# Loading x and the first weights on one queue, and adding and scaling several tiles at once at the end, in a two-layer recurrent decoder on one core

## The chip, the cores and the metric

The kernel runs on one core of a Trainium2 chip. The core has five engines that run side by side: PE (TensorE, matmuls, with weight loads shown as PEld), DVE (VectorE), ACT (ScalarE), POOL (GpSimd) and SP (SyncE, which here only issues transfers). The metric is the device time of one execution in microseconds (us), as a median over runs. TensorE's granted clock is 0.998 over the profiled execution.

## The reference, cut to what matters

The input x is 256 positions of 2048 features, float32. Two layers follow each other, each with a gated convolutional FFN behind it, and a last norm:

```python
for layer in range(DEPTH):                       # DEPTH = 2
    if layer % 2 == 0:
        x = rglru_rwkv7_layer(x, even_norm[e], even_w_in[e], ...)
    else:
        x = mlstm_layer(x, odd_norm[o], odd_w_in[o], ...)
    x = conv_ffn(x, ffn_norm[layer], ffn_w_gate[layer], ffn_w_up[layer], ...)
return rms_norm(x, final_norm)

def rms_norm(x, g):
    y = x32 * lax.rsqrt(jnp.mean(x32 * x32, axis=-1, keepdims=True) + EPS)
    return (y * g).astype(x.dtype)

def conv_ffn(x, norm, w_gate, w_up, conv_w, conv_b, w_down):
    h = rms_norm(x, norm)
    u = jax.nn.silu(causal_dwconv(h @ w_gate, conv_w, conv_b)) * (h @ w_up)
    return x + u @ w_down
```

The even layer normalizes x and multiplies it by `even_w_in`; its last 288 output columns are the low-rank inputs of the RWKV-7 half (decay, in-context rate and gate), and the kernel computes these first. All else of the layers is untouched by the change.

## The kernel before, in words

**Layout.** Features lie on the 128 partitions and the 256 positions along the free axis, so x is 16 tiles of 128 x 256, called the residual: one buffer `res_sb` of 128 x 16 x 256, whose tiles are `res[k]`.

**Precision.** Every float32 operand is split in two: a rounded part made by ACT (a copy or a scaled copy) and the remainder made by DVE (a subtraction). A product takes the rounded weights with both parts of x, and the weights' remainder with the rounded part of x. Lines 254 and 255 split weights (`wh`, `wl` from `raw`), lines 378 and 379 make the operands `x` of the residual and multiply the norm's gain in. The factor 1/rms comes only behind the matmuls: it is one value for each position, the square sums are gathered in `ssq` (ACT squares at L392, DVE adds at L394), two small matmuls (L405) add them over the partitions, POOL raises to the power -1/2 (L416), two more matmuls (L432) spread the result over all partitions, and ACT copies it to `rstd` (L434, shown as `bc`).

**Weights** come from memory in chunks of up to 1 MB into the tile `raw`, which has two buffers, all issued by SP. A chunk can be issued only when its buffer has been read out by the split.

**The start.** The constructor loads the constants `con` (identity and ones) on POOL's queue. `load_x` (L148) loads the gain vector and then x on ACT's queue, in pieces of 1, 1, 2, 4, 4 and 4 tiles (L160, L163), and beside it the low-rank weights `elow` on SP's queue: group 0 in three pieces (L161), groups 1, 2 and 3 whole (through `raw_load`, L235). A group holds the weights of four k-tiles, 4 x 288 columns. Behind group 1 SP loads the vectors (`vec`, L192). `warm(7)` runs seven matmuls on zeros, two instructions each (L146), and then come 16 k-tiles of three products of three matmuls each (L270 to L272, outputs `pc`, `pc`, `pw`). Behind that the program loads `con_even` (L512, recorded at L204) on SP and begins the wide projection of the even layer (weights `ein`, output `mm`, the same lines). For each of the eight head groups j it loads `lora` (L542: on SP for j = 0, else POOL), `a_w` (L544, POOL) and, inside the head group's own sequence, `gate` (L753, POOL). The work of `gate` for j = 0 begins with an ACT cast at L805, that of `lora` at L610.

**Order.** The program text gives the order only as a preference. A scheduler walks through it, and an engine (or a queue) takes the first instruction in the text that can go; one that must wait for a buffer is passed by later ones. The order on each engine that comes out is fixed and cannot change at run time.

**The FFN** (L472) has an up-projection (`flat_pairs` over `fgu`, L346 and L348) and a down-projection (`fd`, same lines), which yields one pair of output tiles after another: a PSUM tile of 128 x 2 x 2 x 256, the first 2 for the two output tiles, the second 2 for the two parts that are to be added. For each tile `add_residual` (L465) adds both parts to the residual on DVE (L467), makes the next layer's operand (not in the last FFN) and the square; in the last FFN ACT then scales the tile by the final gain (L372).

**The end.** Behind the last pair come the square sum, the power and the spread, and then a loop over the 16 tiles (L1171): two of three tiles are multiplied by `rstd` on DVE and the third on POOL, and each time three tiles are done SP stores them (L1174), the last tile alone.

Of the kernel before, what the change touches and what calls it, by code (L numbers as in the profile page):

```python
# [17 lines left out]
F32 = mybir.dt.float32  # L18
F32R = mybir.dt.float32r
AF = mybir.ActivationFunctionType  # L20
ALU = mybir.AluOpType
# [3 lines left out]
P = 128  # L25
T = 256
D = 2048
KD = D // P
# [87 lines left out]
class Builder:  # L116
    def __init__(self, tc, io, ctx):
        self.tc, self.nc, self.io = tc, tc.nc, io
        self.tile_pool = lambda **k: tc.tile_pool(reuse_waits="tile", **k)
        nc = self.nc  # L120
        self.n = 0
        pool = lambda name, bufs, **k: ctx.enter_context(self.tile_pool(name=name, bufs=bufs, **k))
        self.const = pool("const", 1)
        self.raw = pool("raw", 2)
        self.parts = pool("parts", 2)

        self.short = pool("short", 1)
        self.act = pool("act", 1)
        self.mm_ps = pool("mm_ps", 3, space=PSUM)
        self.vec_sb = self.const.tile([P, NV], F32, name="vec_sb")  # L130
        self.cons = {}
        self.load_con("con", self.const)
        self.x = [None] * KD
        self.sumsq = None
        self.rstd = None
        self.tasks = []
        self.norm_psum = lambda: self.psum_mm()[:, 0]

    def warm(self, n):

        nc = self.nc
        z = self.act.tile([P, 2 * T], F32, name="warm", tag="x15")
        nc.vector.memset(z, 0.0)
        ps = self.psum_mm()
        for i in range(n):
            nc.tensor.matmul(ps, z[:, 0:P], z, start=True, stop=True)  # L146

    def load_x(self, gain, low, outs):  # L148

        nc = self.nc  # L150
        res = self.act.tile([P, KD, T], F32, name="res")
        self.res_sb = res
        self.res = [res[:, k] for k in range(KD)]
        g = VOFF[gain]
        nc.scalar.dma_start(out=self.vec(gain, 0, KD), in_=self.io["vec"][:, g:g + KD])
        w = sum(n for _, n in outs)
        first = [0, 1, 2, 4]
        raw = self.raw_tile(4 * w)
        for a, b in zip(first, first[1:]):
            nc.scalar.dma_start(out=res[:, a:b], in_=self.io["xT"][:, a:b])  # L160
            nc.sync.dma_start(out=raw[:, a * w:b * w], in_=low[0][:, a * w:b * w])  # L161
        for i in range(1, 4):
            nc.scalar.dma_start(out=res[:, 4 * i:4 * i + 4], in_=self.io["xT"][:, 4 * i:4 * i + 4])  # L163
        self.warm(7)
        for i in range(4):
            raw = raw if i == 0 else self.raw_load(low[i], 4 * w)
            if i == 1:
                self.load_vec(gain)
            hi, lo, piece = self.parts_of(raw, 4)
            for k in range(4 * i, 4 * i + 4):  # L170
                self.operand(k, gain)
                piece(k % 4)
                c = k % 4 * w
                for ps, n in outs:
                    self.mm3(ps[0:n], (hi, lo), slice(c, c + n), self.x[k], k == 0, k == KD - 1)
                    c += n
        self.rstd = None
        self.start(self.squares())
# [188 lines left out]
    def norm_tile(self, k, gain):  # L367
        if gain is not None:
            self.operand(k, gain)
        self.square(k)  # L370
        if gain is None:
            self.nc.scalar.activation(self.res[k], self.res[k], AF.Copy, scale=self.vec("final_norm", k))  # L372

    def operand(self, k, gain):
        nc, a = self.nc, self.act
# [89 lines left out]
    def add_residual(self, m, ps, gain):  # L465
        for i in range(2):
            self.nc.vector.tensor_tensor(out=self.res[m], in0=ps[:, i], in1=self.res[m], op=ALU.add)  # L467
        if gain is not False:
            self.norm_tile(m, gain)


    def ffn(self, l, gain):  # L472
        nc, tc = self.nc, self.tc
        with ExitStack() as es:
# [15 lines left out]
                ux.append(big.tile([P, 2, T], F32R, name=self.name("ux"), tag=f"u{f}"))  # L490
                self.split(u, ux[f])
            for m, ps in enumerate(self.flat_pairs(self.io[f"fd{l}"], NF, KD // 2, ux, pps)):
                for i in range(2):
                    self.add_residual(2 * m + i, ps[:, i], gain)


    def even(self, gain):
        nc, tc = self.nc, self.tc
        with ExitStack() as es:
# [10 lines left out]
            low = [(self.pc(P, T), P), (self.pc(P, T), P), (self.pw(P, T), 32)]  # L510
            self.load_x("even_norm", self.io["elow"], low)
            self.load_con("con_even", E, nc.sync)  # L512
            ps = self.projections(ein, 40, EWIDE)
# [24 lines left out]
            ps = chain([ahead], ps)  # L538
            pairs, lru = [], []
            for j in range(8):  # L540
                lw = self.wt("lora", P, 2, P, bufs=1)
                (nc.gpsimd if j else nc.sync).dma_start(out=lw, in_=self.io["lora"][j, :, 0:2])  # L542
                lru_w = self.wt("lru_w", P, 2, P, bufs=1)
                nc.gpsimd.dma_start(out=lru_w, in_=self.io["a_w"][j])  # L544
                k, r, v = (self.shifted(self.W, next(ps), 3 + 3 * j + i, t)
                           for i, t in enumerate("krv"))
                if j == 0:
# [48 lines left out]
    def rwkv_pair(self, j, lw, low, r, k, v, out):  # L596

        nc = self.nc
# [34 lines left out]
        ps = self.pw(P, T)  # L633
# [116 lines left out]
            V.tensor_tensor(out=tt, in0=ps, in1=zt, op=ALU.add)  # L750
            yield from wait(WAITS[8])
        gw = once("gate", P, 2, P)
        nc.gpsimd.dma_start(out=gw, in_=self.io["lora"][j, :, 2:])  # L753

        ps = self.pw(P, NCK, 2, CHUNK)
        for c in range(NCK):
# [397 lines left out]
    def build(self):  # L1154
# [11 lines left out]
        self.norm_psum = lambda: self.psum_mm()[:, 0]  # L1166
        self.norm_end()
        self.finish(*self.tasks)
        for k in range(KD):
            e = nc.gpsimd if k % 3 == 2 else nc.vector  # L1170
            e.tensor_tensor(out=self.res[k], in0=self.res[k], in1=self.rstd, op=ALU.mult)  # L1171
            if k % 3 == 2 or k == KD - 1:
                o = k - k % 3
                nc.sync.dma_start(out=self.io["out"][:, o:k + 1], in_=self.res_sb[:, o:k + 1])  # L1174


@with_exitstack
# [108 lines left out]
```

## Time and profile before

| | us |
|---|---|
| median of three runs | 2606.73 |
| lowest and highest | 2604.91, 2606.99 |
| the profiled execution | 2604.45 |
| its span | 2602.6 |
| PE busy in it | 2567.6 |
| DVE, ACT, POOL busy | 1869.0, 1470.6, 142.5 |
| moved between memory and chip | 454.41 MB |

The profile is of one execution. A row of a group or of the timeline reads: start and busy time in us, engine, line of the kernel, operation, what it writes and reads by the program's names, shape, count, and in brackets the idle time of the engine just before and what ended it. PE's spans are modelled and overlap: what counts is the distance from one start to the next. SPq, ACTq and POOLq are the engines' instruction queues, where transfers are issued. A row of transfers gives the issuing queue, the count, the size of one and the median time from issue to landing. In the chain of waits a row is start, length and what ran; a row with DMA is a transfer from issue to landing. Only the ends of the span are looked at here: about the first 50 us, and the 17 us behind the last large matmul.

### The profile page before, as it was taken

The page shows a single profiled execution, that of the slowest core. Times are in us where ns is not written, and L with a number is a line of the kernel's source. Part 1 is how long each engine was busy: PE and PEld are TensorE (multiplying, and loading weights), DVE is VectorE, ACT ScalarE, POOL GpSimd, SP SyncE. Part 2 cuts the span into 40 slices and gives each one's busy share as a digit, 9 for nine tenths or more (in the row PEclk, how much of TensorE's full clock was granted, in tenths as well). Part 3 has the DMA queues.
Part 4 walks back from the last instruction along what each step waited for, and adds up shares of the span by engine and source line. Part 5 has one row for each costly group of instructions (what it writes and reads, how often), then busy time and mean ns, then how long its engine had stood idle before and what let it go on. Part 6 is the DMA issues. An engine that isn't in the chain of part 4 may idle for free.

```text
span 2602.6 us, 43142 instructions
## 1 busy us (share of the span) xinstructions
PE 2567.6 (99%) x16438; PEld 2264.4 (87%) x16438; DVE 1869.0 (72%) x4205; ACT 1470.6 (57%) x3071; POOL 142.5 (5%) x402
## 2 busy tenths in 40 slices
PE   9999999999999999999999999999999999999997
PEld 8888887888888888888888888888888888888886
DVE  7988888988777775555777788865677777775554
ACT  7766663655555554444666777644555555554443
POOL 1222121000000000000010000000000000000000
PEclk9999999999999999999999999999999999999999
DMA  6434334565555555555444344455555555555553
GB/s 210 158 109 139 122 105 148 181 221 207 190 187 191 193 194 194 195 179 197 162 147 146 130 146 164 144 197 192 185 189 193 194 194 194 187 188 192 191 197 130
DMA packets 67696, 454.41 MB, mean 175 GB/s; under 512 B 9328, under 2 KB 10352, under 8 KB 14240
## 3 DMA queue, kind: packets, MB, share of 16 engines
q1 hardware_dynamic: 62064, 441.69, 48.8%
q0 software_dynamic: 4416, 7.85, 1.1%
q8 instruction: 129, 2.11, 0.3%
q10 hardware_dynamic: 1008, 2.11, 0.2%
q14 instruction: 79, 0.65, 0.1%
HBM read 448.70 MB, written 2.10 MB: 173 GB/s over the span
## 4 chain that ended last, share of the span: by engine, by line
PE 79%; issue 11%; DVE 6%; ACT 2%; DMA 1%; POOL 1%; ACTq 0%; DVEq 0%; POOLq 0%
PE mp L346 30%; PE mm L333 20%; PE mp L348 15%; PE mm L270 2%; PE mm L271 1%; PE mm L272 1%; PE mm L268 1%; DVE wl L255 1%; PE mm L266 1%; PE sc L986 1%; PE pv L971 1%; PE pz L1126 1%; DMA blocks<-dc 1%; PE pr L980 0%; POOL rsq L416 0%
## 5 line engine op out<-in xcount | busy, mean ns | idle before, releaser
L255 DVE TENSOR_TENSOR wl<-raw,wh 128x512 fp32r<-128x512 f32 (+1 forms) x1680 | 1092.0, 684 | 521.3 <-ACT wh L254 517.9
L254 ACT CAST wh<-raw 128x512 fp32r<-128x512 f32 (+1 forms) x1680 | 955.5, 617 | 696.2 <-PE mp L346 530.2
L346 PE MATMUL mp<-x,wh 128*128 128x512 f32 x2816 | 874.1, 392 | 0.0
L348 PEld LDWEIGHTS mp<-x,wl 128*128 128x128 f32 x2816 | 528.8, 188 | 116.4
L348 PE MATMUL mp<-x,wl 128*128 128x256 f32 x2816 | 555.7, 279 | 0.0
L346 PE MATMUL mp<-ux,wh 128*128 128x512 f32 x1408 | 436.8, 392 | 0.0
L346 PEld LDWEIGHTS mp<-x,wh 128*128 128x128 f32 x2816 | 426.5, 188 | 0.1
L333 PE MATMUL mm<-x,wh 128*128 128x512 f32 x1024 | 333.8, 406 | 0.0
L348 PEld LDWEIGHTS mp<-ux,wl 128*128 128x128 f32 x1408 | 264.4, 188 | 58.1
L348 PE MATMUL mp<-ux,wl 128*128 128x256 f32 x1408 | 277.9, 279 | 0.0
L333 PEld LDWEIGHTS mm<-x,wl 128*128 128x128 f32 x1024 | 192.2, 188 | 42.8 <-issue 0.2
L346 PEld LDWEIGHTS mp<-ux,wh 128*128 128x128 f32 x1408 | 213.2, 188 | 0.0
L333 PE MATMUL mm<-x,wl 128*128 128x256 f32 x1024 | 205.8, 280 | 0.0
L270 PE MATMUL mm<-x,wh 128*128 128x256 f32 x640 | 188.8, 295 | 0.0
L272 PE MATMUL mm<-x,wl 128*128 128x256 f32 x640 | 179.2, 280 | 1.8 <-DVE wl L255 1.8
L271 PE MATMUL mm<-x,wh 128*128 128x256 f32 x640 | 179.5, 281 | 0.0
L333 PEld LDWEIGHTS mm<-x,wh 128*128 128x128 f32 x1024 | 158.9, 188 | 5.3 <-ACT z L459 2.7
L333 PE MATMUL mm<-yx,wh 128*128 128x512 f32 x512 | 160.4, 392 | 0.0
L270 PEld LDWEIGHTS mm<-x,wh 128*128 128x128 f32 x640 | 120.1, 188 | 6.5 <-issue 0.9
L272 PEld LDWEIGHTS mm<-x,wl 128*128 128x128 f32 x640 | 120.0, 187 | 2.4 <-DVE wl L255 2.2
L271 PEld LDWEIGHTS mm<-x,wh 128*128 128x128 f32 x640 | 120.3, 188 | 0.7
L333 PEld LDWEIGHTS mm<-yx,wl 128*128 128x128 f32 x512 | 96.2, 188 | 19.9
(362 smaller groups left out, 2752.3 us busy)
## 6 DMA issues: line engine op xcount, KB each, us to landing
raw<-fgu SPq DMA_DIRECT2D x176, 1024.0 KB, 4.8
raw<-fd SPq DMA_DIRECT2D x88, 1024.0 KB, 4.8
raw<-ein SPq DMA_DIRECT2D x40, 1024.0 KB, 4.9
raw<-oxm SPq DMA_DIRECT2D x32, 1024.0 KB, 4.8
raw<-oz SPq DMA_DIRECT2D x32, 1024.0 KB, 4.9
raw<-oout SPq DMA_DIRECT2D x32, 1024.0 KB, 4.8
raw<-eoa SPq DMA_DIRECT2D x8, 1024.0 KB, 4.9
raw<-eob SPq DMA_DIRECT2D x8, 1024.0 KB, 4.9
```

Of the source, the lines that this page charges most:

```text
L254: nc.scalar.copy(hi[:, s], raw[:, s])
L255: nc.vector.tensor_tensor(out=lo[:, s], in0=raw[:, s], in1=hi[:, s].bitcast(F32), op=ALU.subtract)
L266: TE.matmul(ps[:, 1], lo, x[:, 1], start=False, stop=False)
L268: TE.matmul(ps, hi, x, start=False, stop=stop)
L270: TE.matmul(ps, hi, x[:, 0], start=start, stop=False)
L271: TE.matmul(ps, hi, x[:, 1], start=False, stop=False)
L272: TE.matmul(ps, lo, x[:, 1], start=False, stop=stop)
L333: TE.matmul(out, lhsT, rhs, start=start, stop=stop)
L346: TE.matmul(ps[:, i], hi[i], x, start=start, stop=False)
L348: TE.matmul(ps[:, i, 1], lo[i], x[:, 1], start=False, stop=stop)
L971: TE.matmul(ps[:, s], xm[:, 3 + s * P:3 + s * P + P], bv, start=True, stop=True)
L986: TE.matmul(st["sc"][s], xc[:, s * P:s * P + P], r[:, s * P:], start=q == 0, stop=q == CTILES - 1)
```

## The change

Five edits:

1. `con` is no longer loaded by the constructor on POOL, and `load_x` issues x, the low-rank weights and then `con` and the vectors all on SP: x0, weights 0, x1, weights 1, x2 and x3, weights 2 and 3, x4 to x7, group 1, x8 to x11, x12 to x15, `con`, `vec`. Groups 2 and 3 follow in the text as before. ACT's queue keeps the gain vector.
2. `warm(7)` becomes `warm(3)`, issued ahead of the loads, and `warm` makes a two-column copy on ACT, which loads ACT's table.
3. For j = 0 `a_w` and `gate` are loaded by SP in place of POOL.
4. In the FFNs a pair of output tiles is added by two instructions of 128 x 2 x 256 in place of four of 128 x 256; then both operands, both squares, and in the last FFN both scalings by the final gain.
5. At the end DVE alone multiplies 5, 5, 4 and 2 tiles with one instruction each, with `rstd` repeated over the tiles; the four stores go to SP and ACT in turn.

```diff
@@ Builder.__init__
-        self.load_con("con", self.const)
@@ warm
         nc.vector.memset(z, 0.0)
+
+        t = self.short.tile([P, 2], F32, name="table")
+        nc.vector.memset(t, 0.0)
+        nc.scalar.copy(t[:, 0:1], t[:, 1:2])
@@ load_x
+        self.warm(3)
+
+        queue = nc.sync
         w = sum(n for _, n in outs)
+        load = lambda a, b: queue.dma_start(out=res[:, a:b], in_=self.io["xT"][:, a:b])
         first = [0, 1, 2, 4]
-        raw = self.raw_tile(4 * w)
+        raws = [self.raw_tile(4 * w) for _ in range(2)]
         for a, b in zip(first, first[1:]):
-            nc.scalar.dma_start(out=res[:, a:b], in_=self.io["xT"][:, a:b])
-            nc.sync.dma_start(out=raw[:, a * w:b * w], in_=low[0][:, a * w:b * w])
-        for i in range(1, 4):
-            nc.scalar.dma_start(out=res[:, 4 * i:4 * i + 4], in_=self.io["xT"][:, 4 * i:4 * i + 4])
-        self.warm(7)
+            load(a, b)
+            queue.dma_start(out=raws[0][:, a * w:b * w], in_=low[0][:, a * w:b * w])
+        load(4, 8)
+        queue.dma_start(out=raws[1], in_=low[1])
+        load(8, 12)
+        load(12, KD)
+        self.load_con("con", self.const, queue)
+        self.load_vec(gain)
         for i in range(4):
-            raw = raw if i == 0 else self.raw_load(low[i], 4 * w)
-            if i == 1:
-                self.load_vec(gain)
+            raw = raws[i] if i < 2 else self.raw_load(low[i], 4 * w)
@@ norm_tile
         self.square(k)
-        if gain is None:
-            self.nc.scalar.activation(self.res[k], self.res[k], AF.Copy, scale=self.vec("final_norm", k))
@@ new, behind add_residual
+    def add_pair(self, m, ps, gain):
+        nc = self.nc
+        x, pair = self.res_sb[:, m:m + 2], (m, m + 1)
+        for i in range(2):
+            nc.vector.tensor_tensor(out=x, in0=ps[:, :, i], in1=x, op=ALU.add)
+        if gain is not None:
+            for k in pair:
+                self.operand(k, gain)
+        for k in pair:
+            self.square(k)
+        if gain is None:
+            for k in pair:
+                nc.scalar.activation(self.res[k], self.res[k], AF.Copy, scale=self.vec("final_norm", k))
@@ ffn
-                for i in range(2):
-                    self.add_residual(2 * m + i, ps[:, i], gain)
+                self.add_pair(2 * m, ps, gain)
@@ even
-                nc.gpsimd.dma_start(out=lru_w, in_=self.io["a_w"][j])
+                (nc.gpsimd if j else nc.sync).dma_start(out=lru_w, in_=self.io["a_w"][j])
@@ rwkv_pair
-        nc.gpsimd.dma_start(out=gw, in_=self.io["lora"][j, :, 2:])
+        (nc.gpsimd if j else nc.sync).dma_start(out=gw, in_=self.io["lora"][j, :, 2:])
@@ build
-        for k in range(KD):
-            e = nc.gpsimd if k % 3 == 2 else nc.vector
-            e.tensor_tensor(out=self.res[k], in0=self.res[k], in1=self.rstd, op=ALU.mult)
-            if k % 3 == 2 or k == KD - 1:
-                o = k - k % 3
-                nc.sync.dma_start(out=self.io["out"][:, o:k + 1], in_=self.res_sb[:, o:k + 1])
+        cuts = [0, 5, 10, 14, KD]
+        for i, (o, e) in enumerate(zip(cuts, cuts[1:])):
+            x = self.res_sb[:, o:e]
+            nc.vector.tensor_tensor(out=x, in0=x, in1=self.rstd.unsqueeze(1).to_broadcast([P, e - o, T]), op=ALU.mult)
+            (nc.scalar if i % 2 else nc.sync).dma_start(out=self.io["out"][:, o:e], in_=x)
```

## The prediction

> **What bounds the kernel now.** I read the page first, then the busy time by window of the first 27 us and of the last 17 us, then the timeline of the engines in those two places, because the change touches only the loading at the start, the adds behind the down-projections and the scaling at the end.
>
> ```profile
> span 2602.6 us, 43142 instructions
> PE 2567.6 (99%) x16438; PEld 2264.4 (87%) x16438; DVE 1869.0 (72%) x4205; ACT 1470.6 (57%) x3071; POOL 142.5 (5%) x402
> ```
>
> PE is busy in 2567.6 of 2602.6 us. Only 35 us are open; the change can win what PE idles at the two ends, or spends there on work that is no part of the result.
>
> ```profile
> 1.46 8.81 PE L146 MATMUL mm<-warm 128*128 128x512 f32 x14 [1.46 <-DVE warm L143]
> 18.32 0.28 PE L270 MATMUL pc<-x,wh 128*128 128x256 f32 x1
> 26.48 0.28 PE L270 MATMUL mm<-x,wh 128*128 128x256 f32 x1
> 27.00:40.00 13.00, 12.87 (x109) 12.87 (x110) 12.47 (x39) 9.46 (x22) 0.00 (x0) 1.00 0.54 179
> 2585.38 0.39 PE L348 MATMUL mp<-ux,wl 128*128 128x256 f32 x2
> ```
>
> (In a window's row: its length, then busy time of PE, PEld, DVE, ACT and POOL, granted clock, DMA share, GB/s.) At the end the large matmuls stop at 2585.8, so the last 16.8 us are a tail. At the start PE has warm-up matmuls until 10.3. The low-rank projection behind them is 16 k-tiles of nine matmuls; tile 8 starts at 18.32 and the next projection at 26.48, so a tile takes (26.48 - 18.32) / 8 = 1.02 us, and 16 of them without a gap start at 10.2, just where the warm-up ends. Behind them PE is busy in 12.87 of 13 us. So each microsecond by which the end of this stream (26.48) moves is one of the whole run.
>
> Why it starts so late is in the queues and on ACT:
>
> ```profile
> 3.17 3.26 ACTq L163 DMA_DIRECT2D res<-xT  x3
> 6.46 1.28 ACT L378 ACT_TABLE_LOAD   x1 [6.46 <-DMA res<-xT]
> 7.75 0.51 ACT L378 ACTIVATE x<-res,vec_sb 128x256 fp32r<-128x256 f32 x1
> 8.49 0.51 ACT L378 ACTIVATE x<-res,vec_sb 128x256 fp32r<-128x256 f32 x1
> 0.74 1.33 SPq L161 DMA_DIRECT2D raw<-elow  x3
> 4.01 0.33 SPq L204 DMA_DIRECT2D con_even_sb<-con_even  x1
> 5.91 0.33 SPq L542 DMA_DIRECT2D lora<-lora  x1
> 12.06 4.14 SPq L235 DMA_DIRECT2D raw<-elow  x2
> ```
>
> ACT is held until 6.43 by issuing the last three loads of x; then it loads its table for 1.28 us; only then is the first operand made. And note SP's order: the program asks for weight groups 2 and 3 before con_even and lora, but group 2 must wait until buffer 0 is read out (12.06), and the scheduler has put con_even and lora ahead of it.
>
> **Part 1, the start of the stream.** ACT loses its six loads of x (it keeps the gain vector), and its table is loaded behind a two-column memset, beside the first transfers. The first operand then waits only for data.
>
> ```profile
> raw<-elow SPq DMA_DIRECT2D x1, 144.0 KB, 2.2
> res<-xT ACTq DMA_DIRECT2D x1, 512.0 KB, 9.0
> 6.67 0.19 PEld L146 LDWEIGHTS mm<-warm 128*128 128x128 f32 x1 [0.45 <-issue]
> ```
>
> The first 144 KB on SP landed 2.2 us after issue. With x0 issued at 0.74 and its weights at 1.2, both are in by about 3.5. One operand takes 0.51 us on ACT and about as long again for its remainder on DVE, the weights the like, so PE could start near 5. The warm-up holds it longer: 7 matmuls are 14 instructions, 3 are 6, and the first six took from 1.46 to 6.67, 0.87 us each (the eight after it 3.6 us, 0.45 each). So PE is free at about 6.6: 10.2 - 6.6 = 3.6 us earlier, the most that the start can win, and at full pace just as the real stream begins. Tiles 0 to 7 are fed: ACT makes a tile in 8.49 - 7.75 = 0.74 us against 1.02 on PE, and x4 to x7, which landed 9.0 us after issue while two queues shared the engines, now stand ahead of all that is not needed yet.
>
> **Part 2, group 2 of the weights.** Tile 8 needs it, and there the transfers decide.
>
> ```profile
> 2.00:4.50 2.50, 2.50 (x4) 0.99 (x3) 0.00 (x0) 0.00 (x0) 1.78 (x10) 1.00 0.99 262
> 4.50:6.50 2.00, 2.00 (x3) 0.69 (x3) 0.00 (x0) 0.04 (x1) 0.31 (x1) 1.00 1.06 399
> 6.50:9.00 2.50, 2.50 (x7) 1.13 (x6) 0.70 (x2) 2.49 (x5) 0.00 (x0) 1.00 0.97 328
> 9.00:16.00 7.00, 7.00 (x55) 6.18 (x55) 5.84 (x16) 5.75 (x16) 1.69 (x6) 1.00 1.04 414
> 12.06 5.25 DMA raw<-elow
> 17.41 1.44 ACT L254 CAST wh<-raw 128x288 fp32r<-128x288 f32 x4 [0.60 <-DMA raw<-elow]
> 19.47 29.27 SPq L235 DMA_DIRECT2D raw<-ein  x7
> 23.87 0.39 ACT L805 CAST gh<-gate 128x256 fp32r<-128x256 f32 x1
> ```
>
> From 2 to 16 us the DMA engines are full (share 0.97 to 1.06). They moved 0.66 + 0.80 + 0.82 + 2.90 = 5.2 MB, which is all that the code asks for up to group 2: x 2.10, three weight groups at 0.59, vec 0.40, con_even 0.46, and con, lora, a_w and gate at 0.13 each, 5.25 MB. Group 2 landed at 12.06 + 5.25 = 17.31, ACT was waiting for it, and PE came to tile 8 at 18.32, 1.0 us later. So the middle of the stream is bound by bytes already, and an earlier start helps only if fewer bytes, or faster ones, stand ahead of group 2.
>
> In the new text con_even, lora, a_w and gate (the last two now on SP) follow groups 2 and 3, but they need no freed buffer, and group 2 does. SP comes to con_even after 12 issues of 0.33 to 0.44 us, at some 5.5 us, and could issue all four by 7. Buffer 0 is read out at 8 at the earliest (1.1 MB for tiles 0 to 3 need until about 6 at the pace of the first rows, then two tiles of 0.74). So I expect the scheduler to do again what SP's order shows, and put all four ahead of group 2. Then the same 5.25 MB stand up to its end. What may be won is pace: at 262 and 328 instead of 414 GB/s, 2.5 x (1 - 262/414) + 2.5 x (1 - 328/414) = 1.4 us were lost. The rows of x and weights stay as short at the start, and only three loads leave POOL's queue, so I take a third, 0.5 us (bounds 1.4, and -0.3 if one queue feeds the engines a little worse than three). Group 2 lands at 16.8, tile 8 starts at 17.8, the stream ends at 26.0: **0.5 us** of the 3.6 is left, and PE idles from 6.6 + 8 x 1.02 = 14.8 to 17.8.
>
> The Trainium skill ("Trainium Kernel Development and Optimization", Key Constraints) says that transfers from the SP, ACT and POOL queues run on the same 16 engines and interleave, and that several issuers save only issue time. The DMA share above agrees; by that rule the move by itself wins nothing in transfer. The skill's "DMA: Bandwidth & Descriptors" (Specifications) gives a core about 358 GB/s from HBM; the row of 9 to 16 us has 414, and the measurement decides.
>
> Behind: group 3 follows group 2 by 0.59 / 0.414 = 1.4 us, PE needs it 4.1 us later; the first ein load went out 2.2 us after group 2 landed (19.47) and was needed 9.2 us after (26.48): no new wait. The gate's load now stands on SP among loads that wait for buffers, and its cast, at 23.87 in ACT's order, is ahead of the casts for ein. If it came late, ACT, DVE and PE would wait; its own buffer is free, so I cost it at nothing (up to 2 us if it falls behind an ein load).
>
> **Part 3, the pairs.** All pairs but one have matmuls beside them, also at the seam from the first FFN to the odd layer, where PE takes operands 14 and 15 last:
>
> ```profile
> 1225.00:1230.00 5.00, 5.00 (x30) 4.38 (x30) 4.16 (x10) 3.49 (x8) 0.68 (x6) 1.00 0.44 185
> 2585.80 1.67 DVE L467 TENSOR_TENSOR res<-mp,res 128x256 f32<-128x256 f32 x4 [8.12 <-PE mp L348]
> 2586.72 0.42 ACT L392 ACTIVATE sq<-res 128x256 f32<-128x256 f32 x1 [9.99 <-DVE res L467]
> 2588.02 0.42 DVE L394 TENSOR_TENSOR ssq<-ssq,sq 128x256 f32<-128x256 f32 x1 [0.21 <-ACT sq L392]
> 2569.67 2.50 DVE L255 TENSOR_TENSOR wl<-raw,wh 128x512 fp32r<-128x512 f32 x4 [3.02 <-ACT wh L254]
> 27.24 0.72 ACT L392 ACTIVATE sq<-res 128x256 f32<-128x256 f32 x2
> ```
>
> The last pair of the second FFN is on the path. Four adds of 256 columns take 1.67 us; two of 512, at 0.63 to 0.69 each (2.50 for four such), about 1.35. But the first square starts at 2586.72, after two of the four adds; now it waits for both, to 2587.2. Two squares in 0.72 us end at 2587.95, the last sum starts at 2588.0 against 2588.02: **0** (bounds 0.3 worse, 0.2 better).
>
> **Part 4, the scaling.**
>
> ```profile
> 2592.12 6.41 DVE L1171 TENSOR_TENSOR res<-res,bc 128x256 f32<-128x256 f32 x11 [1.53 <-ACT bc L434]
> 2593.50 5.75 SPq L1174 DMA_DIRECT2D out<-res  x6
> 2594.00:2595.50 1.50, 0.00 (x0) 0.00 (x0) 1.50 (x3) 0.00 (x0) 1.50 (x2) 0.50 0.67 262
> 2599.00:2601.00 2.00, 0.00 (x0) 0.00 (x0) 0.00 (x0) 0.00 (x0) 0.00 (x0) 0.50 1.01 386
> 2601.30:2602.60 1.30, 0.00 (x0) 0.00 (x0) 0.00 (x0) 0.00 (x0) 0.00 (x0) 0.50 0.00 0
> L690 DVE TENSOR_TENSOR zo<-pw,con_even_sb x16: 403/413/428, 77.1 to 389.0; 64x256 f32<-64x256 f32 x16
> ```
>
> Now the scaling lasts until 2598.5 and the 2.10 MB of output go out with holes (a share of 0.67 at 2594, 1.01 at the end); the last byte moves at 2601.3, 1.3 us before the end. Afterwards DVE does 5, 5, 4 and 2 tiles alone: by 0.63 us for 512 columns about 1.5, 1.5, 1.2 and 0.6 us, ready at 2593.6, 2595.1, 2596.3 and 2596.9. A repeated operand costs DVE nothing that shows (L690 has one: 0.41 us for 256 columns, as plain adds have). If bytes start 0.8 us after the first issue, at 2594.4, and five tiles need 1.6 us to go out, each group is ready before the one ahead is out, and the output is one transfer of 2.10 / 0.40 = 5.3 us, to 2599.7. With the 1.3 us the end is at 2601.0: **1.6 us** less (bounds 1.1, with one hole of 0.5 us, and 2.0 at 414 GB/s and an earlier start).
>
> **Sum.** 0.5 + 0 + 1.6 = 2.1 us. The profiled execution is 2604.45 (span 2602.6 and 1.85 around it) and becomes 2602.3; it lay 2.3 below the median of 2606.73. From the median: 2604.6. With all bounds, 2603.1 to 2606.2.
>
> **Rivals.** *Constants really behind.* If groups 2 and 3 precede con_even, lora, a_w and gate on SP, 0.85 MB less stand ahead: 0.85 / 0.414 = 2.1 us more, tile 8 at 15.7, near PE's own pace of 14.8. The start wins 2.6 (at most 3.6), the total is 4.2: 2602.5, at best 2601.1. For it speaks the text's order, and that SP has more to issue; against it SP's order in before.
>
> *The clock falls in the gap.* This ends on the other side.
>
> ```profile
> 2586.00:2592.00 6.00, 1.83 (x8) 1.45 (x8) 2.81 (x9) 2.03 (x5) 0.69 (x1) 0.87 0.00 0
> 66.76 1.13 PE L870 MATMUL pw<-lru_x,lru_w 128*128 128x256 f32 x4 [0.99 <-DVE lru_x L444]
> ```
>
> Its place is the gap before tile 8, 3.0 us by my sum. At the end of the run the granted clock averages 0.87 over the six us after the matmuls stop and is 0.50 from 2594 on: full for 6 x (0.87 - 0.50) / 0.50 = 4.4 us, so until 2590.4, 4.6 us after the last large matmul, with eight small ones between. If it fell in the gap, tiles 8 and on would run at half pace for the 5.2 us that the warm-up needed: 2.6 us lost, in all 0.5 slower than before, 2607.2. It decides from a gap of somewhere between 3 and 4.6 us. The skill's "TensorE: Matmul & The Clock Gate" (Part 1) puts the limit at an idle window of about 3.4 us; the trace agrees so far as the 1.0 us idle at 66.8 is followed by matmuls of the usual pace.
>
> *The order elsewhere drifts.* All engines are ordered anew; the even stage has short waits (0.99 us in the row above) that could come out some us either way.
>
> **How the numbers follow.** Forecast 0.45, constants behind 0.30, clock 0.10, drift 0.15 (a third of it faster by over 5 us, a third slower). The measurement of this kernel can tell 0.2%, 5.2 us, from no change. Below 2601.5 lie somewhat under half of the second case and a part of drift: 0.19. Above 2611.9 only drift: 0.05. The rest, 0.76, lies within. The range takes in the first two cases with their bounds and the clock's value: 2601.0 to 2607.4.
>
> **What would show it.** Right: first L270 near 6.6; con_even, lora, a_w and gate on SP ahead of the third elow group; a PE wait of about 3 us before tile 8; the first ein matmul near 26; output without a hole, and the end 15.2 us after the last L348 instead of 16.8. Wrong: the third group ahead of con_even and ein at 23 to 24; half pace behind the gap; ACT waiting for the gate; a 5-tile scaling of much over 1.5 us; or a stage between 50 and 2580 us whose length changed by over 1 us.

## The result, and the profile after

The change made the kernel slower. On one chip the kernel before took 2606.04 us (median of 4 runs, the three of the table above and one more) and the changed kernel 2650.53 (4 runs, 2649.25 to 2654.32): a ratio of 1.0171, 95% interval 1.0159 to 1.0183. I had forecast 2604.6. The profiled execution took 2651.07 us; its granted clock was 0.996, against 0.998, a difference of 0.2% only.

The head of the page of the changed kernel:

```profile
span 2649.3 us, 43083 instructions
PE 2614.7 (99%) x16430; PEld 2286.5 (86%) x16430; DVE 1867.6 (70%) x4167; ACT 1464.8 (55%) x3072; POOL 138.5 (5%) x394
```

The span grew by 2649.3 - 2602.6 = 46.7 us. PE was busy 2614.7 - 2567.6 = 47.1 us longer, with eight instructions fewer. So PE did not wait longer: it needed longer for the same matmuls. The stages show where. The first spread of the norm's factor (the copy `bc`) and the last large matmul stand in the timelines of before and of after as follows (start, busy time, instruction):

```profile
49.29 0.37 ACT L434 COPY bc<-pw 128x256 f32<-128x256 f32 x1 [3.06 <-PE pw L432]
```

```profile
52.70 0.37 ACT L440 COPY bc<-pw 128x256 f32<-128x256 f32 x1 [3.14 <-PE pw L438]
2632.91 0.40 PE L356 MATMUL mp<-ux,wl 128*128 128x256 f32 x2
```

The start lost 52.70 - 49.29 = 3.4 us. From there to the last large matmul it took 2632.91 - 52.70 = 2580.2 us, against 2585.38 - 49.29 = 2536.1: **44.1 us** more. The tail is 17.22 - 16.39 = 0.8 us shorter. 3.4 + 44.1 - 0.8 = 46.7. Nearly all of the loss lies between the two places that the prediction looked at, in code in which the diff changes nothing but the additions behind the down-projections.

It is not spread evenly. Each FFN, from its first to its last matmul, took 729.5 us before and 746.9 after, 17.5 more (2.4%). The stretch from `bc` to the first FFN lost 3.0 of 447 us (0.7%) and that between the two FFNs 6.2 of 631 (1.0%); why these lost less isn't shown. In the timelines of before and of after the second FFN begins with these rows:

```profile
1856.02 0.63 PE L346 MATMUL mp<-x,wh 128*128 128x512 f32 x2
```

```profile
1886.10 0.63 PE L354 MATMUL mp<-x,wh 128*128 128x512 f32 x2
```

Inside it, in the up-projection, two `wh` matmuls and two `wl` matmuls, one step, follow each other over and over. Three steps lie between the two rows, first of before, then of after:

```profile
2299.95 0.62 PE L346 MATMUL mp<-x,wh 128*128 128x512 f32 x2
...
2302.02 0.62 PE L346 MATMUL mp<-x,wh 128*128 128x512 f32 x2
```

```profile
2346.95 0.63 PE L354 MATMUL mp<-x,wh 128*128 128x512 f32 x2
...
2349.07 0.63 PE L354 MATMUL mp<-x,wh 128*128 128x512 f32 x2
```

They take 2.07 us before and 2.12 after. Over all rows between 2290 and 2330 us (57 and 56 steps) the mean is 0.690 and 0.707 us, 2.4% more. No engine is waited for in these rows. The groups of both kernels by line, operation and shape (busy us, mean ns of one, idle us before them):

```profile
L346 PE MATMUL mp<-x,wh 128*128 128x512 f32 x2816 | 874.1, 392 | 0.0
L348 PE MATMUL mp<-x,wl 128*128 128x256 f32 x2816 | 555.7, 279 | 0.0
```

```profile
L354 PE MATMUL mp<-x,wh 128*128 128x512 f32 x2816 | 885.5, 395 | 0.0
L356 PE MATMUL mp<-x,wl 128*128 128x256 f32 x2816 | 564.3, 281 | 0.0
```

The mean length of one (392 and 395 ns) hides most of it, since neighbours overlap. The distance of the starts is the figure to read.

What differs between the two programs for such a matmul is not its order or its shape but where its operand lies. `warm` got an 8-byte tile, `table`, in the pool `short`. It takes a slot of 32 bytes in every partition, and what is allocated behind that pool lies 32 bytes further on. In the built programs the residual begins at byte 70016 of a partition before and at 70048 after, the first operand at 86400 and 86432; both `wh` (37184) and `wl` (53568) stay. Counted modulo 128, operands went from 0 to 32 and the weights stayed at 64.

### The profile page after: what moved, and what is told of

Same layout as the page of the kernel before. It is cut to its first block, busy times and chain, and to the rows that moved or that the text cites. A ratio compares the mean times of both kernels' runs of the same rounds, so it can differ in the third digit from the quotient of the medians.

```text
span 2649.3 us, 43083 instructions
## 1 busy us (share of the span) xinstructions
PE 2614.7 (99%) x16430; PEld 2286.5 (86%) x16430; DVE 1867.6 (70%) x4167; ACT 1464.8 (55%) x3072; POOL 138.5 (5%) x394
## 4 chain that ended last, share of the span: by engine, by line
PE 79%; issue 11%; DVE 6%; DMA 1%; ACT 1%; POOL 1%; SPq 0%; DVEq 0%; POOLq 0%; ACTq 0%
PE mp L354 30%; PE mm L341 20%; PE mp L356 15%; PE mm L278 2%; PE mm L280 1%; PE mm L279 1%; PE mm L276 1%; DVE wl L263 1%; PE mm L274 1%; PE sc L1006 1%; DMA blocks<-dc 1%; PE pv L991 1%; PE pz L1146 1%; PE pr L1000 0%; PE pw L724 0%
## 5 line engine op out<-in xcount | busy, mean ns | idle before, releaser
L354 PE MATMUL mp<-x,wh 128*128 128x512 f32 x2816 | 885.5, 395 | 0.0
L356 PE MATMUL mp<-x,wl 128*128 128x256 f32 x2816 | 564.3, 281 | 0.0
L354 PE MATMUL mp<-ux,wh 128*128 128x512 f32 x1408 | 442.6, 395 | 0.0
L354 PEld LDWEIGHTS mp<-x,wh 128*128 128x128 f32 x2816 | 434.4, 187 | 0.1
```

The source lines that it names most:

```text
L354: TE.matmul(ps[:, i], hi[i], x, start=start, stop=False)
L356: TE.matmul(ps[:, i, 1], lo[i], x[:, 1], start=False, stop=stop)
```

## The experiments

**Theory A: the place.** The shift of 32 bytes makes the matmuls slower. **Rival B: the order.** The new loads, queues or the order on the engines do it. The rest of the change was to be settled beside it. Each run is timed against the kernel before on the same chip; the results are in tables, as the median in us with its ratio to before and the 95% interval, and the span of the profile. `w` is the address of `wh` and `wl` modulo 128, `x` that of the operands, the distance is x - w modulo 128.

**1. The changed kernel with the table in a place that exists.** Order and instructions are those of the changed kernel; the addresses are those of before.

```diff
-        t = self.short.tile([P, 2], F32, name="table")
+        t = self.short.tile([P, 2], F32, name="table", tag="ms")
```

> The changed kernel, with the two-column tile of the table load put into a slot that is there already (that of ms), so that no tile behind it moves: the order on every engine is that of the changed kernel, and the addresses are those of the kernel before. Theory A, address: the 8-byte tile moved the residual and all matmul operands by 32 bytes, from multiples of 64 to 32 beyond one, and each matmul then costs 2 to 4% more; without it the 44 us between 50 and 2633 us go, the start stays some 2 to 3.5 us later and the tail 0.8 us shorter: 2606 to 2610. Rival B, order, queues or clock (the new order, or the clock that falls at 14 us, leaves PE slower for the rest of the run): it stays at 2648 to 2654.

**2. The kernel before, with the tile alone.** The 32 bytes and a memset are added, and nothing else of the change; in the second kernel the tile is 40 bytes and shifts by 64.

```diff
@@ warm, kernel before: shift of 32
+        t = self.short.tile([P, 2], F32, name="table")
+        nc.vector.memset(t, 0.0)
@@ the same, shift of 64
+        t = self.short.tile([P, 10], F32, name="table")
+        nc.vector.memset(t, 0.0)
```

> The kernel before, with an 8-byte tile ahead of the others in its pool and one small memset for it; PE's order is that of the kernel before. Theory A: about 44 us slower, 2648 to 2654, spread over all stages with matmuls. Rival B: as before, 2604 to 2608.

> The kernel before, with a 40-byte tile there, so that the operands move by 64 bytes (they keep a multiple of 64, but no longer of 128). Theory A with a grain of 64 bytes: as before, 2604 to 2608. With a grain of 128: 2625 to 2654. Rival B: as before.

**3. Weights shifted too.** A further 8-byte tile in the first pool moves weights and operands by 32, on top of the shift in `short`: w = 96, x = 64.

```diff
@@ warm, kernel before
+        t = self.short.tile([P, 2], F32, name="table")
+        nc.vector.memset(t, 0.0)
+        u = self.const.tile([P, 2], F32, name="shift")
+        nc.vector.memset(u, 0.0)
```

> The kernel before, with an 8-byte tile ahead of the weight buffers and another behind them: raw weights, wh and wl lie 32 bytes beyond a multiple of 64, the operands of the residual on a multiple of 64. Theory A1, only what matmuls stream (the moving operand) counts: 2604 to 2609. A2, every read by PE counts, weight loads too: 2630 or more. Rival B: as before.

| kernel | w | x | distance | median | ratio | span |
|---|---|---|---|---|---|---|
| before | 64 | 0 | 64 | 2606.0 | 1 | 2602.6 |
| after | 64 | 32 | 96 | 2650.53 | 1.0171 (1.0159 to 1.0183) | 2649.3 |
| 1, table in place | 64 | 0 | 64 | 2607.78 | 1.0007 (0.9998 to 1.0016) | 2604.9 |
| 2, shift of 32 | 64 | 32 | 96 | 2649.3 | 1.0162 (1.0147 to 1.0178) | 2648.5 |
| 2, shift of 64 | 64 | 64 | 0 | 2625.89 | 1.0074 (1.0061 to 1.0088) | 2622.5 |
| 3, weights shifted too | 96 | 64 | 96 | 2649.44 | 1.0166 (1.0152 to 1.0179) | 2647.6 |

The head of the page of experiment 1:

```profile
span 2604.9 us, 43083 instructions
PE 2567.5 (99%) x16430; PEld 2265.0 (87%) x16430; DVE 1865.3 (72%) x4167; ACT 1464.7 (56%) x3072; POOL 138.5 (5%) x394
```

The same 43083 instructions, and PE is back at 2567.5 us from 2614.7. With the whole change in place and only the tile elsewhere, the loss is gone; with the tile alone in the kernel before, it is there. Theory A is shown, rival B fell. But what I had thought of the addresses fell as well: a shift of 64 is not free, so it isn't that operands must lie on a multiple of 64 bytes, and 3 shows that the address of the operands alone doesn't decide: x = 64 cost 20 us in the second kernel of 2 and 43 in that of 3.

**4. Which places are good.** The first guess was that weights at 0 as well would be better than before, or at least no worse. The pool `short` moves ahead of `raw`, in the kernel before and in the changed one (there with the table in place). This puts the weights at 0 and leaves the operands at 0.

```diff
+        self.short = pool("short", 1)
         self.raw = pool("raw", 2)
         self.parts = pool("parts", 2)
...
-        self.short = pool("short", 1)
         self.act = pool("act", 1)
```

> The kernel before, with the small pool (64 bytes) put ahead of the weight buffers: the weights wh and wl, which lay 64 bytes beyond a multiple of 128, move to a multiple of 128; the operands of the residual stay where they are, and the order on every engine is the same. Theory A2 (every read of PE pays for its address, with a grain of 128 bytes, as the operands at 64 cost 20 us): 2580 to 2596. Theory A1 (only the streamed operand counts, or weight loads are hidden): 2604 to 2608.

> The changed kernel with the table's tile in the slot of ms and the small pool ahead of the weight buffers: weights and operands both on multiples of 128. Theory A2: the run of the changed kernel in place (2607.8) less what the weights at 128 bring to the kernel before, 2582 to 2598. Theory A1: 2606 to 2610.

Both became slower, by as much as the shift of 64 had made it. The first of them has the instructions of the kernel before, in the same order on every engine, so its 19 us are the addresses alone. What these share with it is the distance: 0. This was **theory C**: the distance of operands and weights modulo 128 counts, not the place of either. Four kernels more put the same distances elsewhere, all from the kernel before; the second one without the moved pool.

```diff
@@ w 0, x 64: the pool moved, and
+        pad = self.act.tile([P, 16], F32, name="pad")
+        nc.vector.memset(pad, 0.0)
@@ w 96, x 32: the pool as before, and
+        pad = self.const.tile([P, 2], F32, name="pad")
+        nc.vector.memset(pad, 0.0)
@@ w 32, x 32: the pool moved, and
+        pad = self.const.tile([P, 2], F32, name="pad")
+        nc.vector.memset(pad, 0.0)
@@ w 0, x 32: the pool moved, and
+        pad = self.act.tile([P, 2], F32, name="pad")
+        nc.vector.memset(pad, 0.0)
```

> The kernel before, order unchanged, weights wh and wl at 0 and operands at 64 beyond a multiple of 128 (before: 64 and 0). Theory C, only the distance between weights and operands modulo 128 counts, 64 is free, 0 costs 20 us and 32 or 96 some 43: 2604 to 2608. Rival D, each address counts for itself (weights want 64, operands want 0, each 20 us): about 2645.

> The kernel before, weights at 96 and operands at 32 modulo 128: distance 64, but neither on a multiple of 64. Theory C: 2604 to 2608. Rival E, any address off a multiple of 64 costs by itself: 2640 to 2670.

> The kernel before, weights and operands both at 32 modulo 128: distance 0. Theory C: 2622 to 2629, as with both at 0 or both at 64. Rival E: 2640 to 2670.

> The kernel before, weights at 0 and operands at 32 modulo 128: distance 32, the one of the four not yet run (the changed kernel has 96). Theory C: between 2620 and 2655, and about 2649 if 32 and 96 are alike. Rival E: 2640 to 2655 as well.

| kernel | w | x | distance | step, us | median | ratio |
|---|---|---|---|---|---|---|
| before, pool moved | 0 | 0 | 0 | 0.697 | 2625.03 | 1.0073 (1.0059 to 1.0087) |
| table in place, pool moved | 0 | 0 | 0 | 0.697 | 2625.01 | 1.0074 (1.006 to 1.0087) |
| w 0, x 64 | 0 | 64 | 64 | 0.690 | 2605.57 | 0.9998 (0.9988 to 1.0007) |
| w 96, x 32 | 96 | 32 | 64 | 0.690 | 2607.14 | 1.0 (0.9991 to 1.0009) |
| w 32, x 32 | 32 | 32 | 0 | 0.697 | 2625.75 | 1.0073 (1.0058 to 1.0088) |
| w 0, x 32 | 0 | 32 | 32 | 0.693 | 2613.7 | 1.003 (1.002 to 1.004) |

The timelines of PE between 2299 and 2303 us, first of w 32, x 32, then of w 0, x 64; four steps lie between the two rows:

```profile
2299.77 0.63 PE L348 MATMUL mp<-x,wh 128*128 128x512 f32 x2
...
2302.56 0.63 PE L348 MATMUL mp<-x,wh 128*128 128x512 f32 x2
```

```profile
2299.80 0.62 PE L348 MATMUL mp<-x,wh 128*128 128x512 f32 x2
...
2302.56 0.62 PE L348 MATMUL mp<-x,wh 128*128 128x512 f32 x2
```

2.79 us against 2.76. An added tile with its memset costs nothing by itself: w 96, x 32 has one, at distance 64. Over all kernels so far: distance 64 costs nothing that can be told (three kernels beside the one before), 0 costs 19 to 20 us (four), 96 costs 42 to 45 (three), wherever the tiles lie. Of the distance 32 there is one kernel, and it costs 7.6 us (2613.7 against 2606.1): I had guessed it to be like 96, and that missed.

**5. Which of the two weights?** From the kernel before, with operands at 64. A pad of 64 bytes between the two weight tiles puts one of them at distance 0 from the operands and leaves the other at 64.

```diff
@@ parts_of, kernel before
         hi = self.parts.tile([P, n], F32R, name=self.name("wh"), tag="wh")
+        if self.n_pad == 0:
+            self.n_pad = 1
+            pad = self.parts.tile([P, 16], F32, name="pad", tag="pad", bufs=1)
+            nc.vector.memset(pad, 0.0)
@@ the other way round: the lines of hi stand behind those of the pad and of wl's tile
```

In the first kernel wh lies at 64 and wl at 0, so that wh is at distance 0; in the second wh lies at 0 and wl at 64, so that wl is.

> The kernel before, order unchanged; operands at 64, rounded weights wh at 64 (distance 0), remainders wl at 0 (distance 64) modulo 128. If each weight load collides with the stream beside it alike, half of the 20 us: 2613 to 2619. If only loads of wh collide: 2624 to 2628; if only loads of wl: 2604 to 2608.

> The counterpart: wl at distance 0, wh at distance 64. Half each: 2613 to 2619. Only wh: 2604 to 2608. Only wl: 2624 to 2628.

| kernel | wh | wl | x | step, us | median | ratio |
|---|---|---|---|---|---|---|
| wh at distance 0 | 64 | 0 | 64 | 0.705 | 2643.43 | 1.0143 (1.0129 to 1.0157) |
| wl at distance 0 | 0 | 64 | 64 | 0.703 | 2643.02 | 1.0136 (1.0122 to 1.015) |

PE's timeline in the first of them, again four steps between the rows, 2.83 us:

```profile
2299.64 0.63 PE L351 MATMUL mp<-x,wh 128*128 128x512 f32 x2
...
2302.47 0.63 PE L351 MATMUL mp<-x,wh 128*128 128x512 f32 x2
```

All that I had expected missed. Both weights at distance 0 cost 19 to 20 us; one of them costs 35 to 37, whichever it is. So a sum over pairs of one weight tile and its operand doesn't explain the loss: that `wh` and `wl` lie in different halves of 128 bytes costs by itself, even with one of them at the free distance. Theory C holds only as a rule found here for weights that lie alike. Which reads meet each other, and why 64 is free, isn't settled.

**6. The end alone.** The kernel before with edits 4 and 5 (pairs, scaling, stores), and the start of before.

> The kernel before with the pairs and the scaling of the changed kernel (edits 4 and 5), nothing at the start, all addresses as before. By the trace of the changed kernel its tail, from the last large matmuls on, is 0.8 us shorter: 2604.5 to 2606. By the prediction's sum 1.6 us shorter: 2604.4. If the order of adds and squares inside the first FFN costs something at the seam: above 2606.

2606.06 us (11 runs), ratio 1.0002 (0.9993 to 1.0011), span 2602.4: nothing that can be told from no change.

**7. The start.** The changed kernel with the table in place, and then: x on ACT's queue instead of SP's; the same with the warm-up of before; the warm-up of before alone.

```diff
@@ x on ACT's queue
-        load = lambda a, b: queue.dma_start(out=res[:, a:b], in_=self.io["xT"][:, a:b])
+        load = lambda a, b: nc.scalar.dma_start(out=res[:, a:b], in_=self.io["xT"][:, a:b])
@@ longer warm-up
-        self.warm(3)
+        self.warm(7)
```

> The changed kernel with addresses in place and the loads of x back on ACT's queue; weights, con and vectors stay on SP, warm-up 3, table load early. Theory Q (one queue delivers the first tiles too slowly, and the order that follows from it puts eight operands and squares ahead of group 2's cast): the start is better than that of the changed kernel in place by 1 to 3 us, 2604.5 to 2607. Rival W (three warm-up matmuls end too early whatever the queue, PE idles before the first tiles): no better, 2607 to 2609.

> The kernel of c3 (changed kernel in place, x on ACT's queue) with seven warm-up matmuls in place of three: PE comes to the first tiles later and should have no long gap before group 2. Theory K (the clock that fell in c3 cost the start its gain): granted clock 1.00 between 18 and 24 us, the first ein matmul at 26 to 26.6 instead of 28.1, span 2601 to 2602 instead of 2602.9. Rival L (group 2's arrival and what follows it decide, the clock's fall lies beside another wait): the first ein matmul stays at 28 or later.

> The changed kernel in place with seven warm-up matmuls. There the clock did not fall in the profile, and eight operands and three squares stand ahead of group 2's cast on ACT. Theory M (that order decides; PE waits anyway): no change against the changed kernel in place, first ein matmul at 27.3 and span about 2605. Rival (the early stream is worth what PE wins by it): 3 us later, about 2608.

| kernel, table in place | first ein matmul | `bc` copied | median | ratio | span |
|---|---|---|---|---|---|
| kernel before | 26.48 | 49.29 | 2606.0 | 1 | 2602.6 |
| after itself, table not in place | 28.86 | 52.70 | 2650.53 | 1.0171 | 2649.3 |
| x on SP, 3 (experiment 1) | 27.28 | 50.70 | 2607.78 | 1.0007 (0.9998 to 1.0016) | 2604.9 |
| x on ACT, 3 | 28.14 | 50.20 | 2605.68 | 1.0001 (0.9992 to 1.001) | 2602.9 |
| x on ACT, 7 | 26.50 | 48.61 | 2603.96 | 0.9989 (0.998 to 0.9998) | 2602.9 |
| x on SP, 7 | 28.29 | 51.65 | 2607.14 | 1.0001 (0.9992 to 1.001) | 2604.6 |

Of x on ACT with 3, the time fell in the range of theory Q, 2604.5 to 2607, but not by the start that Q rested on: `bc` came 0.5 us earlier than in experiment 1, not 1 to 3, and the first ein matmul 0.9 later.

In the profiles of the two kernels with x on ACT the clock makes the difference at the start. The windows (length, busy time of PE, PEld, DVE, ACT and POOL, granted clock, DMA share, GB/s) and the first matmul of tile 8, with 3 and with 7 warm-up matmuls:

```profile
17.96 0.38 PE L278 MATMUL pc<-x,wh 128*128 128x256 f32 x1 [1.55 <-ACT wh L262]
18.00:24.00 6.00, 6.00 (x36) 5.57 (x37) 5.75 (x15) 5.93 (x20) 0.14 (x1) 0.72 0.53 178
```

```profile
17.93 0.39 PE L278 MATMUL pc<-x,wh 128*128 128x256 f32 x1 [0.28 <-ACT wh L262]
18.00:24.00 6.00, 6.00 (x50) 5.71 (x51) 5.79 (x15) 6.00 (x20) 0.78 (x1) 1.00 0.59 186
```

Tile 8 starts at the same time in both, 17.9, for its weights come no sooner. With the short warm-up PE idled for 1.55 us before it and the clock fell (36 matmuls in six us instead of 50, and the first ein matmul 1.6 us later); with the long one the gap was 0.28 us and the clock stayed. Theory K held for the start; its span was to be 2601 to 2602 and was 2602.9, no shorter than without it. The trace shows where the rest went. In this execution the clock was at half from 103.9 to 107.4 us, and between 100 and 112 us the run fell back by 1.6 us against before (3.4 us at half pace make 1.7). In the profile of before the clock fell only in the tail. The windows of before and of x on ACT with 7:

```profile
100.00:112.00 12.00, 10.27 (x79) 9.45 (x78) 11.65 (x39) 9.85 (x22) 3.78 (x9) 1.00 0.57 184
```

```profile
100.00:112.00 12.00, 9.99 (x64) 9.08 (x63) 10.43 (x35) 9.41 (x21) 3.59 (x8) 0.86 0.64 199
```

With x on SP the longer warm-up brings nothing to the median; the first ein matmul came 1.0 us later than theory M had it. x on ACT with 7 is the best version that I ran: 2603.96 against 2606.77 of before on that chip, 0.1% faster, an interval just clear of 1 and less than the 0.2% that I had set as what the measurement can tell. Its `bc` is 0.7 us earlier than that of before and its tail 0.8 shorter, but the one profile of it lost 1.8 us between the two, 1.6 of them at the clock's fall near 104. Of the other executions only the mean clock is on record, so that the median's gain isn't put down to one stage.

## Why the prediction was wrong

**The step that failed** is in part 1: ACT's table "is loaded behind a two-column memset", and the sum has no term for the tile that this memset writes. I costed the instructions of `warm` and put the place of the tile at nothing, without a reason. Its 32 bytes cost 42 us (a ratio of 1.0162 with nothing else changed, experiment 2), twenty times the sum of all that I worked out. My sum had no term for the 2536 us between the ends; the case "the order elsewhere drifts" gave a twentieth of the chance to a loss of over 5 us there, and for another reason. The line that I had named as a sign of being wrong, a stage between 50 and 2580 us whose length changed by over 1 us, is what came: 17.5 in each FFN, 44.1 in all.

**Part 1, the start of the stream:** right for the first matmul, which came at 5.96 us, forecast 6.6; the table's load stood at 1.18. "Tiles 0 to 7 are fed" was wrong: PE waited before tile 4, and nothing of the early start reached the end of the stream.

**Part 2, SP's order:** wrong. I took the order of before as evidence that the constants would pass group 2 again. SP's timeline of after:

```profile
9.63 5.69 SPq L243 DMA_DIRECT2D raw<-elow  x2
15.38 0.42 SPq L212 DMA_DIRECT2D con_even_sb<-con_even  x1
15.85 0.42 SPq L562 DMA_DIRECT2D lora<-lora  x1
16.32 0.57 SPq L564 DMA_DIRECT2D lru_w<-a_w  x1
21.96 2.67 SPq L243 DMA_DIRECT2D raw<-ein  x2
24.68 0.42 SPq L773 DMA_DIRECT2D gate<-lora  x1
```

Groups 2 and 3 wait at 9.63 and con_even, lora and a_w stand behind them: my rival's order. With x on ACT's queue the constants went ahead of group 2, so that my reading of SP fits that shape and not this one. The rival promised 2.6 us at the start, and the start lost 3.4 at `bc` and 2.4 at the first ein matmul. Its own terms failed. The windows of after, and then its gap on PE, the landing of x4 to x7, ACT's order and the first ein matmul:

```profile
2.00:4.50 2.50, 2.50 (x4) 1.00 (x3) 0.61 (x2) 1.95 (x6) 0.00 (x0) 1.00 0.91 261
4.50:6.50 2.00, 2.00 (x4) 0.69 (x3) 1.65 (x5) 1.61 (x5) 0.00 (x0) 1.00 0.84 277
6.50:9.00 2.50, 2.50 (x18) 2.21 (x17) 1.36 (x4) 1.28 (x5) 0.00 (x0) 1.00 0.97 262
14.00:18.00 4.00, 4.00 (x23) 3.80 (x22) 4.00 (x11) 4.00 (x12) 2.29 (x6) 0.57 0.79 295
```

```profile
13.32 0.38 PE L278 MATMUL pc<-x,wh 128*128 128x256 f32 x1 [1.84 <-ACT wh L262]
3.54 7.37 DMA res<-xT
14.50 3.28 ACT L384 ACTIVATE x<-res,vec_sb 128x256 fp32r<-128x256 f32 x8
19.76 1.42 ACT L262 CAST wh<-raw 128x288 fp32r<-128x288 f32 x4
28.86 0.28 PE L278 MATMUL mm<-x,wh 128*128 128x256 f32 x1
```

First, the pace. I took a third of 1.4 us as won; from 4.5 to 9 us the transfers moved 277 and 262 GB/s where before had 399 and 328. 2 x 0.122 + 2.5 x 0.066 = 0.41 MB less, 1.0 us at 0.414: worse than my bound of -0.3. In experiment 1, the same order, they moved 350 and 304, by the same sum 0.4 us lost, so the pace differs by execution. Second, the gap came four tiles earlier than I had it. x4 to x7, issued at 3.54, landed 7.37 us later, at 10.91, and group 1 behind them at 12.32. ACT made the four operands first and cast group 1 at 12.86, and PE waited 1.84 us for that cast, until 13.32. Third, ACT's order puts the operands of x8 to x15 and squares ahead of group 2's cast. That cast ran at 19.76, though group 2 had landed at 17.64, and PE waited 0.87 us for it before tile 8, at 20.23. So the order on ACT, with DVE's remainders and sums beside it, was the bound there, not the landing of group 2. Fourth, the first ein load, which I had put down as "no new wait", was issued at 21.96 instead of 19.47, and PE waited 0.91 us for the remainder made of it, against 0.3 in before.

The clock fell behind the first gap, to 0.57 over 14 to 18 us. This is the rival "the clock falls in the gap", with its place and its threshold (3 to 4.6 us) both wrong, and its half pace lasted 3.4 us (14.3 to 17.7), not 5.2. It cost nothing that shows at tile 8: PE had done tile 7 and waited. Experiment 1 bears this out. There the clock stayed at 1.00 in that window and in the next, behind a gap of 2.45 us before tile 8. x4 to x7 landed at 9.27 and group 1 at 10.69, 1.6 us earlier than in after; tile 8 and the first ein matmul (18.60 and 27.28) are 1.6 earlier as well, so the difference between the two starts stands in these landings and not in the clock. The start still lost 1.4 us against before, read at `bc`:

```profile
14.00:18.00 4.00, 2.15 (x19) 1.84 (x17) 3.88 (x12) 3.68 (x12) 2.84 (x7) 1.00 0.92 316
18.00:24.00 6.00, 5.40 (x46) 5.24 (x47) 5.94 (x18) 4.84 (x15) 1.19 (x2) 1.00 0.55 191
18.60 0.38 PE L278 MATMUL pc<-x,wh 128*128 128x256 f32 x1 [2.45 <-ACT wh L262]
```

Whether the clock falls behind such a gap differed between these executions; I have one profile of each.

**Part 3, the pairs:** forecast 0 (0.3 worse to 0.2 better). In the kernel with the end alone, from the start of the last large matmul to the square sum's small ones it took 2588.93 - 2585.59 = 3.34 us against 2588.50 - 2585.38 = 3.12 in before: 0.2 worse, within the bounds. The first square starts later than I had it, 0.04 us behind both adds, and two sums of 0.96 us follow instead of one of 0.42:

```profile
2633.35 1.41 DVE L482 TENSOR_TENSOR res<-mp,res 128x512 f32<-128x512 f32 x2 [8.39 <-PE mp L356]
2634.80 0.72 ACT L398 ACTIVATE sq<-res 128x256 f32<-128x256 f32 x2 [10.81 <-DVE res L482]
2635.24 0.96 DVE L400 TENSOR_TENSOR ssq<-ssq,sq 128x256 f32<-128x256 f32 x2 [0.48 <-ACT sq L398]
2636.25 1.01 PE L411 MATMUL mm<-con_sb,ssq 128*128 128x1 f32 x4 [2.94 <-DVE ssq L400]
```

**Part 4, the scaling:** right, nearly to its size. DVE's and the transfers' rows of after:

```profile
2640.28 4.63 DVE L1192 TENSOR_TENSOR res<-res,bc 128x1280 f32<-128x1280 f32 x4 [1.53 <-ACT bc L440]
2642.00:2643.00 1.00, 0.00 (x0) 0.00 (x0) 1.00 (x1) 0.00 (x0) 0.00 (x0) 0.50 0.40 164
2643.00:2644.00 1.00, 0.00 (x0) 0.00 (x0) 1.00 (x2) 0.00 (x0) 0.00 (x0) 0.50 1.02 410
2646.00:2647.00 1.00, 0.00 (x0) 0.00 (x0) 0.00 (x0) 0.00 (x0) 0.00 (x0) 0.50 1.04 418
2647.00:2648.00 1.00, 0.00 (x0) 0.00 (x0) 0.00 (x0) 0.00 (x0) 0.00 (x0) 0.50 0.82 307
```

The output goes out without a hole, and from the first scaling to the end it takes 2649.3 - 2640.28 = 9.02 us, against 2602.6 - 2592.12 = 10.48: 1.46 of the 1.6 us. What came back is ahead of it: 0.2 in the pairs, and 0.4 because the four small matmuls of the square sum took 1.01 us, at half pace, where before had 0.61. The tail as a whole won 0.8 us. In experiment 1 those matmuls took 0.61 and the tail was 15.85 us long, 1.4 less than before; in the kernel with the end alone they took 0.61 too, but the last bytes landed later, and 0.4 were left: from the first scaling to the end it took 9.85 us, 0.6 less than before. Each is one execution.

**The forecast apart from the tile:** with the table in place the ratio is 1.0007 (0.9998 to 1.0016), so a forecast of no difference that can be told would have been right, but mine had the wrong sign: the start lost 1.4 us where I had a gain of 0.5, the tail won 1.4 of 1.6, and the middle of that one profile lost 2.3 (from `bc` at 50.70 to the last large matmul at 2589.05), about 1.7 of it between 100 and 120 us, where the clock fell from 106.2 to 109.6. The median, 2607.78, lies 0.4 above the upper end of my range.

## What to carry to other kernels

A tile, however small, is an edit of every address behind it: before costing its instructions at nothing, compare the addresses of the operands of the hottest matmuls in both programs. If PE is busy longer with no more instructions, read the distance from one matmul's start to the next in the same place of both traces; when it has changed all through a stage in which PE waits for nothing, and the granted clock has not, look at the addresses before the queues and the order. And a PE that begins earlier than its data only moves the gap: a shorter warm-up or an earlier start is worth what the last transfer or the last cast ahead of the stream allows.

## What the runs showed of the hardware that I had not expected

- The pace of these float32 matmuls depends on where weights and operands begin in a partition, modulo 128 bytes: with both weight tiles alike, 0.690 us a step of the second FFN where the operands begin 64 further, 0.693 at 32, 0.697 at 0, 0.707 at 96; with the two weight tiles 64 apart 0.703 and 0.705. Over the run this is 0, 8, 19 to 20, 42 to 45 and 35 to 37 us.
- The granted clock fell to half behind gaps of 1.55 and 1.84 us on PE (0.57 over the window from 14 to 18 us of after, 0.72 over that from 18 to 24 with x on ACT), and did not behind one of 2.45 us in experiment 1 (1.00 from 18 to 24). Before has gaps of 1.53 us at 60.7 and of 1.73 at 102.3 and kept its clock; after has the first of them as well, 1.54 us at 64.1, and there the clock fell at 65.5. Each of these falls lasted 3.4 us. The Trainium skill ("TensorE: Matmul & The Clock Gate", Part 1) puts the limit at an idle window of about 3.4 us and calls the window free-running; the falls here are at shorter gaps than that, and what in the window decides these runs don't show.
- With all loads on SP's queue less was moved early on. From 2 to 9 us it was 1.86 MB in after, 2.06 in experiment 1, the same order, and 1.85 with x on SP and 7 warm-up matmuls; with x on ACT's queue it was 2.27 MB in before, 2.29 with 3 and 2.34 with 7. The output moved at 410 and 418 GB/s in the windows in which the transfer engines were full (1.02 and 1.04).
